# Where a small side job is woven into a large kernel: the sampled tokens' heads move from the first MLP to the second, and the first blocks' head outputs are transposed one stage earlier

## The chip, the core and the metric

The kernel runs on one core of one Trainium2 chip. The metric is device microseconds of one execution, lower being better; the kernel before took 2691.82 us, the median of three runs (2685.82 to 2694.05).

Engines by short names: PE is TensorE, which multiplies matrices; PEld its weight loads; DVE is VectorE, ACT is ScalarE, POOL is GpSimd, SP is the sync engine. SP, ACT and POOL can issue DMA transfers, and an engine's instructions run in the order of its own queue.

## What is computed

One step of a one-layer decoder with two kinds of heads side by side, over a prompt of 2048 tokens and, separately, over 8 × 4 sampled tokens that carry a state. Cut to what matters:

```python
def decoder_layer(x, p, lp, state):
    xn = rms_norm(x, lp['norm_mix_pre'])
    qk_raw, v_m, o_m, gates, q_a, k_a, v_a = split_projection(xn @ lp['w_in'])
    qk, conv_new = short_conv(qk_raw, conv_buf, lp['conv_w'])
    q, k, v, ig, lf = mlstm_heads(qk, v_m, gates, lp['b_gates'])
    if state is None:      # prompt: 16 chunks of 128 tokens
        (c_new, n_new, m_new), h = mlstm_prompt(q, k, v, ig, lf)
        att = swa_prompt(q_a, k_a, v_a, lp['attn_sinks'])
    else:                  # sampled tokens: one chunk of 4, from the state
        (c_new, n_new, m_new), h = mlstm_chunk(init, (q, k, v, ig, lf))
        att, k_new, v_new = swa_sample(q_a, k_a, v_a, k_buf, v_buf, lp['attn_sinks'])
    mix = concatenate([mlstm_output(h, o_m), rms_norm(att)]) @ lp['w_out']
    x = x + rms_norm(mix, lp['norm_mix_post'])
    u = rms_norm(x, lp['norm_ffn_pre'])
    f = square(relu(u @ lp['w_up'])) @ lp['w_down']
    x = x + rms_norm(f, lp['norm_ffn_post'])
    return x + sigmoid(x @ lp['w_pgate']) * (p @ lp['w_pproj'])
```

The mLSTM heads ("memory heads") carry a matrix c (64 × 128 for each of 4 heads), a vector n of 64 and a number m; the attention heads look back 128 tokens, with a key and value cache for the sampled tokens.

## The kernel before

**Stages.** The 16 blocks of 128 prompt tokens are first projected in six chunks (`project`, L615, called at the loop ahead of L1350): gates, keys and values, then queries, the q/k path, and at the end the `v` and the `o` columns, each as eight products per block (one for each 128 rows of the model width). The sampled tokens ride along with the last chunk; their rows go to a DRAM buffer `zsd`. The last blocks then go on in three groups of two chunks each (`GROUPS`): the output projection (`mix_load`, `mix_mm`, `mix_post`), the MLP (`mlp`, 16 steps of 256 hidden columns), and the gated embedding. The head outputs of each block are two DRAM tiles `yd[b]`, written by the heads (`mlstm_chunk` L893, `swa_chunk` L980) and read again by `mix_load`.

Every f32 operand is held as a high and a low part, and one product is three matmuls (`mm3`). Weights go through a ring (`Ring`): the first time a tile is loaded raw, cast on ACT (L248), its low part taken on POOL or DVE (L249), and, if it is used again, kept in DRAM (`keep`, a POOL store `wk<-w`, L268); later uses reload it (`w<-wk`, SP, L274). Which tile is loaded when is written down in `plan` (L383).

**FAST.** MLP step s of group gi is "slow" for s < `FAST[gi]` (L56: 4, 2, 2): 48 matmuls for each of the two chunks, 96 in all. From `FAST[gi]` on it is "fast": `up_both` (L1632) makes both chunks together from seven products of half the size and sums of them, 84 matmuls. The sums of the activations (`sums`, L1585, `last_sum`, L1618, on DVE and ACT) are made once in a group, in step `FAST[gi] − 1`, in memory (`tp`, `wide`) that is taken over there from the load buffers and from decode. The combined weights are made once (`product`, L284 and L413) and kept; a slow step's own weights have keys of their own.

**The side jobs.** `Flow` (L127 on) fixes PE's order while the program is written. It counts a clock of its own in planned microseconds: each matmul adds its columns (times its passes) divided by 2400. Side jobs are generators that issue some work and yield the planned time until they are due again; between products, `tick` (L164) lets those go on that are due, and `drain` (L180) issues all that is left. `swa` and `mls` are the prompt's heads, `tsp` the loads and transposes, `dec` the sampled tokens' heads: `decode` (L1341) waits `DECW` = 20 and then runs `decode_mlstm` (L1070) and `decode_swa` (L1256), whose tiles share memory. Only PE's order (and that of the cache copies, L1089) is kept as written; instructions of other engines may be put ahead in their queues when what they need is there. `reuse_waits="tile"` means that a tile waits for those that held its memory before.

**Around the change.** After the last `project` comes `pe.drain(swa)` (L1350), then the first group's loads are added and drained at once (L1516 and 1517: six y loads on SP, `MIXW` = 6 planned microseconds, then for each of three blocks four transposes and the splits), and only then `mix_mm(0, 0)` begins. `decode` is added at L1543, ahead of the loop over the groups, so it starts in group 0's second output projection (`mix_mm(0, 1)`) and is drained in step `FAST[0] − 1` = 3 (L1724 and 1725). Its loads are issued by ACT (`fetch_small`, L201), among them for each half e and head h

```python
fetch_small(cs[er, :, h, 0:128], c_in[e, h])
fetch_small(cs[er, :, h, 128], n_in[e, h])
```

(L1211 and 1212), where the second writes the 64 elements of n to 64 partitions for four samples; its stores (`put`) go through POOL, and the two copies of the caches (L1089) through SP.

## Time and profile before

| | |
|---|---|
| median of three runs | 2691.82 us |
| profiled execution, its span | 2687.73 us, 2685.6 us |
| last `o` products of the last projection end | 675 us |
| first output projection (`mo`) starts | 693.2 us |
| MLP of group 0: first `up`, first fast step (4) | 797.5 us, 986.1 us |
| second output projection, MLP of group 1 | 1478.7 us, 1549.3 us |
| fast steps of group 1 | 1620.8 us on |

Times are from the start of the span of one profiled execution. A row of a group or of the timeline has the engine, the line of the code, what is written and read (`dn<-w,hh` is a tile `dn` made from `w` and `hh`, buffer numbers left out) and behind "x" a count. In brackets stands how long the engine was idle before, and what ended the wait. A row that ends in "q", such as SPq or ACTq, is an engine's queue at work on issuing DMAs. Names of tiles: `mo` output projection, `up` and `dn` the MLP's two products, `y` loaded head outputs, `yt` and `ut` their transposed forms, `re`, `hh`, `hl` the hidden values, `f` the sums over the MLP, `ts`, `tl` the sums for the fast steps; decode's tiles begin with `dp` and `da` on PE (`dpk`, `daS` and so on), or with `s` (`scs` is c and n, `skc`, `svc` the caches, `szqa` the queries), and `cb` is its constants.

### The profile page before, as it was taken

Reading aid. Unit: us, or ns where it says so; the run is one execution under the profiler, and the core shown is the slowest. Engines: PE = TensorE matmul, PEld = TensorE weight load, DVE = VectorE, ACT = ScalarE, POOL = GpSimd, SP = SyncE. Lnnn points to the kernel's source line nnn. Section 1 sums busy time; section 2 is a strip of 40 time slices with the busy share of each in tenths; the row PEclk is TensorE's granted clock in tenths of the full one; section 3 lists DMA queues with packets and bytes.
Section 4 is the critical chain, followed back from the end, with each engine's and each line's share of the span. In section 5 each row is a group of like instructions: output and inputs, shape, how many; then the busy total and the mean of one; then the engine's idle time right before and its main releaser. Section 6 shows DMA issues by size and latency. Waiting matters only on the chain.

```text
span 2685.6 us, 39181 instructions
## 1 busy us (share of the span) xinstructions
PE 2546.3 (95%) x14282; PEld 2216.1 (83%) x14282; DVE 1473.3 (55%) x3109; ACT 981.4 (37%) x2163; POOL 613.3 (23%) x894
## 2 busy tenths in 40 slices
PE   6899999999878999999989999999999998999997
PEld 6788878887657788888878888899988878999986
DVE  5675756755554486566663474444446345444453
ACT  4555444544433443334452352222223133222241
POOL 5311111112323156566651113000001010000010
PEclk9899999999889999999989999999999999999999
DMA  8756656667977366666589865555556886777786
GB/s 284 275 200 197 208 175 220 210 212 250 287 247 156 133 218 244 235 235 235 227 301 323 322 213 182 187 190 189 188 189 224 293 327 215 255 259 256 258 293 227
DMA packets 225336, 626.97 MB, mean 233 GB/s; under 512 B 35233, under 2 KB 71445, under 8 KB 225128
## 3 DMA queue, kind: packets, MB, share of 16 engines
q1 hardware_dynamic: 173424, 466.78, 52.2%
q0 software_dynamic: 44176, 154.25, 14.8%
q10 hardware_dynamic: 7544, 3.44, 0.6%
q8 instruction: 113, 1.85, 0.3%
q14 instruction: 79, 0.65, 0.1%
HBM read 470.22 MB, written 155.25 MB: 233 GB/s over the span
## 4 chain that ended last, share of the span: by engine, by line
PE 72%; DMA 9%; DVE 8%; issue 4%; POOL 3%; ACT 3%; ACTq 0%; SPq 0%; POOLq 0%; DVEq 0%
PE up L145 19%; PE dn L145 19%; PE pg L145 6%; PE mo L145 4%; PE v L145 3%; PE o L145 2%; PE qk L145 2%; DMA wk<-w 2%; PE gv L145 2%; POOL w L249 2%; PE pv L145 1%; PE aT L149 1%; PE aO L145 1%; DMA w<-wk 1%; PE qa L145 1%
## 5 line engine op out<-in xcount | busy, mean ns | idle before, releaser
L145 PE MATMUL dn<-w,hh 128*128 128x512 f32 x1792 | 567.7, 398 | 14.1 <-DVE f L1683 8.9
L145 PEld LDWEIGHTS dn<-w,hh 128*128 128x128 f32 x1792 | 332.7, 189 | 96.7 <-DVE f L1683 15.4
L1683 DVE TENSOR_TENSOR f<-f,dn 128x512 f32<-128x512 f32 x420 | 285.7, 686 | 218.0 <-PE dn L145 217.7
L145 PE MATMUL dn<-w,hl 128*128 128x512 f32 x896 | 354.3, 395 | 0.1
L1647 DVE TENSOR_TENSOR re<-up,re 128x384 f32<-128x384 f32 (+1 forms) x280 | 144.1, 515 | 297.6 <-PE up L145 297.6
L145 PEld LDWEIGHTS dn<-w,hl 128*128 128x128 f32 x896 | 168.9, 189 | 39.9 <-DVE hl L228 0.6
L268 POOL DMA_DIRECT2D wk<-w x242 | 134.1, 555 | 145.6 <-DVE w L249 109.6
L1648 ACT COPY re<-up 128x384 f32<-128x384 f32 (+1 forms) x40 | 17.9, 448 | 383.1 <-PE up L145 383.1
L228 DVE TENSOR_TENSOR hl<-re,hh 128x384 fp32r<-128x384 f32 (+1 forms) x192 | 117.5, 612 | 65.6 <-ACT hh L227 62.0
L1573 ACT ACTIVATE re<-re 128x384 f32<-128x384 f32 (+1 forms) x160 | 78.8, 493 | 179.3 <-DVE re L1647 177.2
L248 ACT CAST w<-wb 128x512 fp32r<-128x512 f32 x98 | 60.8, 621 | 199.2 <-PE dn L145 124.9
L248 ACT CAST w<-wr 128x512 fp32r<-128x512 f32 (+1 forms) x152 | 93.4, 619 | 104.9 <-issue 30.8
L249 POOL TENSOR_TENSOR w<-wr,w 128x512 fp32r<-128x512 f32 (+1 forms) x76 | 102.0, 1342 | 81.8 <-ACT w L248 62.8
L1394 POOL TENSOR_TENSOR f<-f,gffn 128x512 f32<-128x512 f32 x16 | 21.0, 1319 | 415.4 <-ACT j L1392 415.2
L249 POOL TENSOR_TENSOR w<-wb,w 128x512 fp32r<-128x512 f32 x70 | 89.9, 1295 | 100.8 <-ACT w L248 100.3
L249 DVE TENSOR_TENSOR w<-wr,w 128x512 fp32r<-128x512 f32 (+1 forms) x76 | 80.5, 1061 | 44.4 <-ACT w L248 42.4
L1574 ACT ACTIVATE re<-re 128x384 f32<-128x384 f32 (+1 forms) x192 | 94.8, 494 | 5.9
L1002 DVE CUSTOM_DVE_ANT_0 s<-aS,cst,sink 128x256 f32<-128x256 f32 (+1 forms) x128 | 57.1, 472 | 72.4 <-PE aS L145 72.2
L145 PE MATMUL up<-ut00h,w 128*128 128x384 f32 x320 | 88.6, 348 | 8.4 <-ACT f L1681 5.0
L227 ACT CAST hh<-re 128x384 fp32r<-128x384 f32 (+1 forms) x192 | 92.4, 482 | 6.8
L145 PE MATMUL up<-ut01h,w 128*128 128x384 f32 x320 | 89.8, 343 | 4.8 <-ACT re L1573 4.8
L1008 ACT ACTIVATE s<-s,swt 128x257 f32<-128x257 f32 (+1 forms) x128 | 63.3, 496 | 71.6 <-DVE swt L1005 70.4
(1501 smaller groups left out, 6436.3 us busy)
## 6 DMA issues: line engine op xcount, KB each, us to landing
w<-wk SPq DMA_DIRECT2D x678, 512.0 KB, 4.6
wk<-w POOLq DMA_DIRECT2D x238, 512.0 KB, 5.7
wr<-in_w_down_dram SPq DMA_DIRECT2D x64, 256.0 KB, 5.9
wb<-in_w_up_dram SPq DMA_DIRECT2D x28, 512.0 KB, 3.9
w<-wk SPq DMA_DIRECT2D x20, 528.0 KB, 4.2
x<-in_x_prompt_dram SPq DMA_DIRECT2D x16, 512.0 KB, 4.1
xr<-in_x_prompt_dram SPq DMA_DIRECT2D x16, 512.0 KB, 12.7
y<-yd SPq DMA_DIRECT2D x32, 256.0 KB, 6.2
```

Source lines behind the costliest of these rows:

```text
L145: ins = self.pe.matmul(out, lhsT, rhs, start=start, stop=stop)
L227: act.copy(hi, src)
L228: dve.tensor_tensor(lo, src, hi.bitcast(F32), ALU.subtract)
L248: act.copy(hi, src)
L249: (eng or weng()).tensor_tensor(lo, src, hi.bitcast(F32), ALU.subtract)
L268: put(self.kept[key], t.bitcast(U32))
L1002: dve.tensor_tensor_reduce(s_[:, s, lo : 2 * P], pS[:, s, lo:], bias[:, j, lo:], 1.0 if s == 0 else 0.0625, sink[:, h : h + 1], ALU.add, A ...
L1008: act.activation(e_, e_, AF.Exp, bias=nm[:, s : s + 1], accum_out=sm[:, s : s + 1])
L1573: act.activation(t, src, AF.Relu)
L1574: act.square(t, t)
L1647: add = lambda out, a, b: dve.tensor_tensor(out, a, b, ALU.add)
L1683: dve.tensor_tensor(out(i), out(i), ps[i], ALU.add)
```

## The change

1. `FAST` becomes 2, 4, 2: group 0's steps 2 and 3 are fast, group 1's are slow.
2. `decode` is added at the start of group 1's MLP and drained in that group's step 3.
3. The loads of `decode` go through POOL instead of ACT, and the two cache copies through POOL instead of SP. n is loaded in rows of 64 elements, 16 rows for each half, and transposed on PE into its column; on the way out it is transposed back and stored in rows. Two yields of 1.5 are added for these.
4. In the last projection the y loads of blocks 0, 1 and 2 are issued ahead of the `o` columns into the buffers of x, and their memory halves are transposed between the `o` products, where the other chunks transpose the next x; the window halves, which need no transpose, are split behind the projection. The load and drain at L1516 and 1517 go.

```diff
-FAST = 4, 2, 2
+FAST = 2, 4, 2
...
-    dma, put, fetch_small = nc.sync.dma_start, nc.gpsimd.dma_start, nc.scalar.dma_start
+    dma, put = nc.sync.dma_start, nc.gpsimd.dma_start
...
+        last = ci + 1 == len(CHUNKS)
+        nxt = GROUPS[0][0] if last else CHUNKS[ci + 1]
         for nm, zoff in (("v", Z_V), ("o", Z_O)):
-            if nm == "o" and ci + 1 < len(CHUNKS):
-                fetch(ci + 1)
+            if nm == "o":
+                if last:
+                    ys = [load_y(xpool, "x", b) for b in nxt]
+                else:
+                    fetch(ci + 1)
...
-                if nm == "o" and ci + 1 < len(CHUNKS):
-
-                    nxt = CHUNKS[ci + 1]
+                if nm == "o":
+
                     if k == 3:
                         chunk = Chunk(tpA, f"x{ci + 1}")
                     if k > 3 and k - 4 < len(nxt):
-                        transpose_x(chunk, nxt, k - 4, 0, ps_m)
+                        if last:
+                            mix_heads(chunk, k - 4, nxt[k - 4], ys[k - 4])
+                        else:
+                            transpose_x(chunk, nxt, k - 4, 0, ps_m)
...
+        if last:
+            for i, t in enumerate(ys):
+                mix_windows(chunk, i, t)
         return r
+
+    def load_y(pool_, tag, b):
+
+        src = yds if b == "s" else yd[b]
+        t = pool_.tile([P, D], F32, tag=tag, name=f"y_{b}")
+        for e in range(2):
+            dma(t[: src[e].shape[0], e * 512 : e * 512 + 512], src[e])
+        return t
+
+    def mix_heads(x, i, b, t):
+        transpose_split(t[:, 0:512], *x.part(0, slice(i * P, (i + 1) * P)), ps_m, f"yt{b}", g_mix[0])
+
+    def mix_windows(x, i, t):
+        split_gain(*x.part(1, slice(i * P, (i + 1) * P)), t[:, 512:].rearrange("p (j q) -> p j q", j=4), g_mix[1])
...
-        fetch_small(cb, A["const_b"][:, 0:NCB])
+        put(cb, A["const_b"][:, 0:NCB])
...
-            tc.keep_in_program_order(dma(oc[:, 0 : WIN - DT, :], cc[:, DT:WIN, :]))
+            put(oc[:, 0 : WIN - DT, :], cc[:, DT:WIN, :])
...
-        n_in = A["state_mlstm_n"].rearrange("l (k e) h d -> e h d (l k)", e=2)
+        n_in = A["state_mlstm_n"].rearrange("l (k e) h d -> e (l k) h d", e=2)
...
+        nrow = sp.tile([DB // 2 * MH, 2, MK], F32, name="snr")
         for e in range(2):
             er = slice(e * MK, (e + 1) * MK)
             for h in range(MH):
-                fetch_small(cs[er, :, h, 0:128], c_in[e, h])
-                fetch_small(cs[er, :, h, 128], n_in[e, h])
+                put(cs[er, :, h, 0:128], c_in[e, h])
+            for k in range(DB // 2):
+                put(nrow[k * MH : (k + 1) * MH, e], n_in[e, k])
+        yield 1.5
+        pn = psum(ps_s, "dpn")
+        pe.transpose(pn[:, 0:16], nrow.rearrange("p e d -> p (e d)"), ident[:16, :16])
+        dve.tensor_copy(cs[:, :, :, 128], pn[:, 0:16].rearrange("p (k h) -> p k h", k=4))
         yield 1.5
...
                 put(c_out[e, h], cs[er, :, h, 0:128])
-                put(n_out[e, h], cs[er, :, h, 128])
+        ncol = sp.tile([P, 16], F32, name="snc")
+        dve.tensor_copy(ncol.rearrange("p (k h) -> p k h", k=4), cs[:, :, :, 128])
+        yield 1.5
+        pn = psum(ps_s, "dpno")
+        pe.transpose(pn[:16, 0:P], ncol, ident)
+        dve.tensor_copy(nrow.rearrange("p e d -> p (e d)"), pn[:16, 0:P])
+        for e in range(2):
+            for k in range(DB // 2):
+                put(n_out[e, k], nrow[k * MH : (k + 1) * MH, e])
...
-        fetch_small(kc, A["cache_swa_k"].rearrange("l b s k d -> s (l b) (k d)"))
-        fetch_small(vc, A["cache_swa_v"].rearrange("l b s k d -> s (l b) (k d)"))
+        put(kc, A["cache_swa_k"].rearrange("l b s k d -> s (l b) (k d)"))
+        put(vc, A["cache_swa_v"].rearrange("l b s k d -> s (l b) (k d)"))
...
-    tsp.add(mix_load(0, 0, GROUPS[0][0], False))
-    pe.drain(tsp)
+    yt[0] = chunk
     tsp.add(mix_load(0, 1, GROUPS[0][1], False))
     mix_mm(0, 0, GROUPS[0][0], False)
...
-    dec.add(decode())
...
         G = f"{gi}"
+        if gi == 1:
+            dec.add(decode())
```

The other loads in `decode_mlstm` and `decode_swa` change from `fetch_small` to `put` in the same way, and `mix_load` calls the three new functions.

More of the change, by code (lines that the diff above doesn't have):

```diff
@@ L1078, in decode_mlstm @@
         zqk = sp.tile([NS, 512], F32, name="zqk")
-        fetch_small(zqk, zsd[:, Z_QK : Z_QK + 512])
+        put(zqk, zsd[:, Z_QK : Z_QK + 512])
         zg = sp.tile([NS, 2 * MH], F32, name="zg")
-        fetch_small(zg, zsd[:, Z_G : Z_G + 2 * MH])
+        put(zg, zsd[:, Z_G : Z_G + 2 * MH])
         for b in range(DB):
@@ L1177, in decode_mlstm @@
         pool.memset(va[:, :, 129:130], 0.0)
-        fetch_small(va[:, :, 0:128], zsd[:, Z_V : Z_V + 512].rearrange("p (h v) -> p h v", h=MH))
+        put(va[:, :, 0:128], zsd[:, Z_V : Z_V + 512].rearrange("p (h v) -> p h v", h=MH))
         num = sp.tile([NS, MH, 130], F32, name="snum")
@@ L1224, in decode_mlstm @@
         so = sp.tile([NS, 512], F32, name="sso")
-        fetch_small(so, zsd[:, Z_O : Z_O + 512])
+        put(so, zsd[:, Z_O : Z_O + 512])
         act.activation(so, so, AF.Tanh, scale=0.5)
@@ L1258, in decode_swa @@
         bias_s = sp.tile([P, nk], F32, name="bias_s")
-        fetch_small(bias_s, A["const_b"][:, NCB : NCB + nk])
+        put(bias_s, A["const_b"][:, NCB : NCB + nk])
         zqa = sp.tile([NS, 512], F32, name="zqa")
-        fetch_small(zqa, zsd[:, Z_QA : Z_QA + 512])
+        put(zqa, zsd[:, Z_QA : Z_QA + 512])
         zkv = sp.tile([NS, 256], F32, name="zkv")
-        fetch_small(zkv, zsd[:, Z_KA : Z_KA + 256])
+        put(zkv, zsd[:, Z_KA : Z_KA + 256])
         y = sp.tile([NS, 512], F32, name="sya")
@@ L1442, in mix_load @@
             yt["s"] = sp2.tile([P, KT, 2 * NS], F32R, tag="s", name="sy2")
-        todo = [(i, b, lp.tile([P, D], F32, tag="ld", name=f"y_{b}"), yd[b]) for i, b in enumerate(c)]
+        todo = [(i, b, load_y(lp, "ld", b)) for i, b in enumerate(c)]
         if sample:
-            todo.append((None, "s", lp.tile([P, D], F32, tag="ld", name="y_s"), yds))
-        for i, b, t, src in todo:
-            for e in range(2):
-                dma(t[: src[e].shape[0], e * 512 : e * 512 + 512], src[e])
+            todo.append((None, "s", load_y(lp, "ld", "s")))
         yield MIXW
-        for i, b, t, _ in todo:
+        for i, b, t in todo:
             if i is None:
```

12 lines of the change are left out of this document (6 added, 6 removed).

## The prediction

> **What bounds the kernel now.** I read the page first, then PE's waits around the seam between projection and MLP, then a table of stretches, and last the chain of waits and single rows.
>
> ```profile
> span 2685.6 us, 39181 instructions
> PE 2546.3 (95%) x14282; PEld 2216.1 (83%) x14282; DVE 1473.3 (55%) x3109; ACT 981.4 (37%) x2163; POOL 613.3 (23%) x894
> ```
>
> TensorE (PE) is busy for 95% of the span, so the kernel is bound by PE, and only time in which PE stands still or runs at a low clock can be won. The question is where the missing 139 us (2685.6 − 2546.3) lie. PE's waits between 676 and 955 us, the seam and the first MLP steps of group 0 (line, what it waited for: total, times, longest):
>
> ```profile
> PE mo L145 <- DMA w<-wk: 13.4, 1, 13.4
> PE mo L145 <- ACT f L1486: 6.6, 1, 6.6
> PE up L145 <- ACT f L1681: 5.0, 1, 5.0
> PE up L145 <- ACT re L1573: 4.8, 1, 4.8
> PE up L145 <- POOL w L249: 3.4, 1, 3.4
> ```
>
> The same stretch as a table: after the length come the busy times of PE, PE's weight loads, VectorE (DVE), ScalarE (ACT) and GpSimd (POOL), then the granted clock, the DMA share and GB/s. (From 742 to 756 nothing is lost.) The last three rows are ten fast steps of group 0 (4 to 13), and of group 1 step 0 and the thirteen fast steps 2 to 14.
>
> ```profile
> 675.00:693.00 18.00, 11.27 (x78) 8.59 (x77) 10.03 (x31) 7.86 (x23) 8.09 (x12) 0.68 0.97 363
> 693.00:742.00 49.00, 44.95 (x188) 34.33 (x187) 29.41 (x51) 19.84 (x39) 18.62 (x24) 0.94 0.90 263
> 756.00:770.00 14.00, 0.60 (x4) 0.16 (x2) 3.70 (x3) 2.12 (x6) 3.66 (x3) 0.65 0.52 125
> 770.00:797.00 27.00, 20.40 (x78) 15.68 (x79) 9.29 (x40) 9.45 (x19) 7.21 (x9) 0.80 0.74 261
> 797.00:855.00 58.00, 52.51 (x305) 42.99 (x303) 35.35 (x89) 27.91 (x62) 18.93 (x30) 0.98 0.73 184
> 855.00:952.00 97.00, 87.86 (x426) 73.77 (x427) 40.53 (x69) 34.26 (x74) 21.70 (x26) 0.94 0.46 125
> 986.00:1310.00 324.00, 316.03 (x1561) 280.96 (x1560) 200.65 (x270) 131.41 (x241) 202.16 (x221) 1.00 0.64 243
> 1549.00:1587.00 38.00, 36.91 (x193) 32.55 (x193) 34.49 (x58) 23.83 (x44) 3.37 (x6) 1.00 0.67 223
> 1621.00:2029.00 408.00, 408.00 (x2028) 366.31 (x2027) 184.87 (x301) 92.33 (x177) 18.64 (x21) 1.00 0.56 187
> ```
>
> For each row I count as lost the length minus the busy time, plus the busy time times (1 − clock). The first two rows lose 6.7 + 3.6 and 4.1 + 2.7, together 17.1 us: the **seam**. The next four lose 13.6, 10.7, 6.5 and 14.4, together 45.2 us: **decode** (the sampled tokens' heads) beside group 0. Group 1's MLP, which runs without decode, loses 1.1 us in step 0 and nothing in its fast steps. What makes decode so dear shows in what the SP queue waited for, and then in the chain of waits (start, length, what):
>
> ```profile
> SPq L274 <- DMA scs<-in_state_mlstm_n_dram: 26.9, 3, 23.3
> ```
>
> ```profile
> 742.07 10.81 DMA cb<-in_const_b_dram
> ...
> 765.45 4.77 DMA scs<-in_state_mlstm_n_dram
> 770.28 7.53 DMA w<-wk
> ```
>
> The n state is fetched with the head's 64 elements across partitions, 4 bytes apiece. SP's reload of a weight tile (L274) stood 23.3 us behind one such fetch, and PE stood 13.4 us for that tile. The loads of decode are issued by ACT, which meanwhile evacuated nothing: the 6.6 us behind ACT L1486.
>
> **The change, part by part.**
>
> *Seam.* These rows carry it (SP, then PE):
>
> ```profile
> 679.88 4.91 SPq L1448 DMA_DIRECT2D y<-yd  x6
> ...
> 689.75 1.09 PE L149 MATMUL yt0t<-ident,y 128*128 128x128 f32 x4 [2.52 <-DMA y<-yd]
> ...
> 693.19 1.20 PE L145 MATMUL mo<-w,yt00h 128*128 128x512 f32 x2
> ```
>
> Now the first y loads go out only at 679.88, after the projections, and the first landed for 689.75. After the change these six loads stand in the last o projection, before 660, on SP ahead of w_out's loads; the three groups of transposes are only moved (same count), and their splits go onto DVE and ACT, which have room there. The window splits read chunk part 1 and come behind the last o product, but part 1 is first read in the second half of the first output block, 36 products later. So `mo` follows the window attention's last product, about when SP issues its next loads, and starts near 681 instead of 693.2; the last products of the memory heads, ahead of it now, fall among its own. Late next: blocks 3 to 5. Their loads take the very place on SP that y0 to y2 had (679.88), so the first can land near 689.75, while PE, 6 planned us (MIXW) into `mo`, asks for it near 687. I leave 2.5 us for that and 1.5 for the rest: 17.1 − 4 = **13 won**; bounds 8 (block 3 waits as long as block 0 did and the clock falls again) and 17 (all).
>
> *Decode leaves group 0.* The 45.2 us go. Left are group 1's 1.1 us and about as much for the first making of the weights: **43 won**, bounds 35 and 45. Decode's own PE work leaves group 0 and comes back in group 1, where PE is as full, so it cancels; the two short transposes of n that are new are below 1 us.
>
> *FAST.* Steps 2 and 3 become fast in group 0 and slow in group 1. Step parts, from the chain (`up` x96 is a slow step's, x84 a fast one's; `dn` is the same for both):
>
> ```profile
> 1587.42 16.84 PE up L145 x96
> 1604.27 16.70 PE dn L145 x72
> ```
>
> A slow step is 33.5 us; group 1's fast one 408/13 = 31.4; group 0's, which also makes the products, 324/10 = 32.4. Group 0 wins 2 × 1.1, group 1 loses 2 × 2.1: **2 lost**, with as many products in all. The cover in group 0 is POOL, 202 of 324 us busy in the fast steps; if it were gone, the weights would end last, as they do there already for 0.8 us a step.
>
> *Decode's loads change queues.* Thirty-two loads from ACT and two cache copies from SP go to POOL, and n is fetched in rows of 256 bytes and transposed. What would be late is a PE transpose that waits for a landing, with `up` and `dn` queued behind it in PE's fixed order. Rows that bear on it (POOL's idle time in brackets):
>
> ```profile
> 639.73 3.09 POOL L1085 DMA_DIRECT2D out_dram<-zsd  x6
> ...
> 875.34 2.53 ACTq L1272
> ...
> 1597.37 1.28 POOL L298 TENSOR_TENSOR wb<-wb,wb 128x512 f32<-128x512 f32 x1 [39.23 <-DMA wb<-in_w_up_dram]
> ```
>
> The decode puts of line 1085 ran at 639.73, some 100 us ahead of decode's first load at 742.07: what isn't PE's is put forward where its queue is free. POOL stood idle for 39.23 us just where decode now begins, and is busy 3.4 of 38 us in group 1's step 0. At 0.52 (the six puts in 3.09) to 2.53 us each, the 34 cost POOL 18 to 86 us of the 139 that these four steps last. So the first loads are hidden. The attention half's loads can't be put forward, as they reuse the memory half's tiles and stand behind its 16 stores: (16 + 5) × 0.52 is 11 us, and a landing like the 4.77 of scs makes 16, against 16.5 planned us until its first transposes. I take 3 us (0 to 8). In the Trainium skill, the page "DMA: Bandwidth & Descriptors", section "Latency and other measured facts", gives a first byte after about 0.6 us for loads from SP or ACT and about 1 us for POOL's, which speaks against the move. Thirty-two loads by that would be an estimated 13 us if each were exposed; no row here shows the two side by side.
>
> *Decode's end against step 3.* Adding up the planner's own clock: at group 1's step 3, whose start drains decode, 116 planned us have passed since the MLP's start, and decode, which now starts with the MLP (before, in the second half of the output projection, some 45 us earlier), needs 125. What is issued bare is its last tail, with this chain in the trace of before:
>
> ```profile
> 914.20 1.18 ACT L1312 ACTIVATE sss<-sss,sst 128x1056 f32<-128x1056 f32 x1
> ...
> 923.18 2.09 PE daO L145 x18
> ...
> 929.57 0.94 DVE L1596 TENSOR_TENSOR ts<-ut01h,ut00h 128x768 f32<-128x768 f32 x1
> 969.76 1.82 DVE L1630 TENSOR_TENSOR ut01l<-tl,ut01h 128x768 fp32r<-128x768 f32 x2
> ```
>
> PE stands through max, exponential (1.18) and the copies between the last transposes and that product: **4 us** (3 to 8). The sums for the fast steps begin 4 us after decode's last product (929.57 after 923.18 + 2.09) and took until 971.6, 42 us; before, step 4 came 57 us after them, now 33.5 + 2. Of the 42, 26 are the sums' own DVE time (28 operations of 0.94), and product 7, the first to need the last of them, is the fourth of the step, 6 us in. I take 2 us (0 to 8), and 2 (0 to 15) for what I don't see, such as ACT and DVE crowded by decode beside a full PE. Together 3 + 4 + 2 + 2 = **11 lost** in group 1; all lower ends give 3, all upper ends 39.
>
> The sum: −13 − 43 + 2 + 11 = **−43 us**. The profiled execution took 2687.73 us around its span of 2685.6; the median of the three runs, 2691.82, lies 4.1 above it. So 2644.7 for an execution like the profiled one, and **2649 us** as the median.
>
> The clock is half of the seam's story: behind the gap of 13.4 us the clock reads 0.65, then 0.80. By the Trainium skill's page "TensorE: Matmul & The Clock Gate", Part 1, an idle window of about 3.4 us halves the clock until about as long of work, and these rows agree; by it the bare tail, if it is over 3.4 us in one piece, costs an estimated 1.7 us more than I take.
>
> **The rivals.** *(a) Part of the stalls travels.* ACT and DVE do decode's small steps beside a PE that has no slack, and POOL's queue holds the weight splits of steps 2 and 3 behind stores that wait. Half of 45.2, 23 us, in place of the 11, and the seam's lower bound: −8 − 43 + 2 + 23 = −26, so 2666; with 29 of stall, 2672. For it: PE's waits on ACT L1573 and POOL L249 stand in the rows from 797 on, when the n fetches of 765 were past. Against it: POOL's stores of n, single elements too, ran then, and are rows now.
>
> *(b) Slower.* If the loads on POOL aren't put forward but issued where they are used, PE stands for each of six landings (hrow, v, n with c, zqa, kc, vc) at the 10.81 us that cb took: 65 us. −13 − 43 + 2 + 65 = +11, 2703. It decides from 54 us of new stalls on. Against it stands the row at 639.73; for it, that POOL's queue is one line, and one store that waits holds all loads behind it. The Trainium skill's figures above point the same way, but by far less.
>
> *(c) Everything is won.* Seam 17, decode 45, the 2 of FAST, and only the 3 in group 1: −57, 2635. For it: group 1's steps have no lost time.
>
> *(d) The early y loads bring nothing*, because blocks 3 to 5 take over the whole wait: −8 − 43 + 2 + 11 = −38; inside the forecast's range.
>
> **How the numbers follow.** Forecast with (d) 0.65, (a) 0.17, (b) 0.07, (c) 0.11. The forecast's own cases reach from 2635 to 2668 (the upper end with 30 of the 39 us in group 1); to hold 8 in 10, I go from 2632 to 2676, which takes in (c) and (a) and leaves out (b) and the tails. A difference of 0.3%, 8 us, is about what a measurement of this kernel can tell from no change. Faster by more than that: (a), (c) and the forecast without their worst tails, 0.89; within it 0.05, from the tail of (a) and a mild (b); slower 0.06, from (b).
>
> **What would show it.** Right: `mo` starts near 681 with no cold rows behind it; the stretch from `mo`'s start to group 0's step 4 loses under 10 us; no SP wait over 5 us on scs; group 0 has fourteen steps of about 32.4; in group 1, steps 0 to 2 grow by decode's PE work and a gap of 3 to 5 us stands just ahead of step 3's first `up`. Wrong: a PE wait of over 5 us on skc, szqa, snr or scs; group 1's step 4 starting with a gap behind DVE ts; PE waiting on POOL w L249 in group 1.

## The result and the profile after

The changed kernel takes 2694.48 us against 2686.42 for the kernel before (medians of 20 runs each, taken in turn on the same chips): ratio 1.0025, interval 1.0017 to 1.0033. It is 8 us slower where 43 us less were forecast, within the 0.3% that the prediction set as the least that can be told from no change, though the interval itself leaves out 1. The profiled execution took 2696.58 us, its span 2694.8. The page of the kernel after, whole span:

```profile
span 2694.8 us, 39194 instructions
PE 2550.8 (95%) x14284; PEld 2221.0 (82%) x14284; DVE 1475.1 (55%) x3112; ACT 982.1 (36%) x2163; POOL 635.4 (24%) x928
```

PE is busy as before, and 144 us are missing in place of 139. That hides two large movements, which a table of stretches shows. Of the kernel before, group 0's first MLP steps and its output projection, then the same two in group 1:

```profile
693.20:797.50 104.30, 80.25 (x341) 62.11 (x340) 53.94 (x116) 39.02 (x78) 30.95 (x41) 0.88 0.79 245
797.50:986.10 188.60, 173.96 (x898) 147.14 (x897) 104.52 (x195) 77.24 (x160) 55.81 (x70) 0.96 0.57 158
1478.70:1549.30 70.60, 70.60 (x326) 57.76 (x325) 33.56 (x61) 25.17 (x52) 12.62 (x15) 1.00 0.88 316
1549.30:1683.60 134.30, 133.21 (x674) 119.13 (x673) 85.68 (x131) 54.56 (x100) 33.90 (x38) 1.00 0.57 196
```

The same work in the kernel after (seam, output projection, step 0, steps 1 to 3; then group 1's output projection, step 0, steps 1 to 3):

```profile
694.20:710.70 16.50, 9.93 (x68) 7.39 (x66) 12.83 (x33) 7.27 (x18) 6.44 (x8) 0.65 0.98 369
710.70:784.50 73.80, 72.68 (x331) 58.92 (x330) 41.61 (x76) 34.88 (x74) 32.91 (x40) 0.99 0.85 299
784.50:832.20 47.70, 41.80 (x193) 35.38 (x192) 40.19 (x62) 28.15 (x52) 13.32 (x18) 0.89 0.67 234
832.20:930.90 98.70, 97.05 (x481) 86.63 (x480) 63.21 (x82) 39.57 (x73) 55.78 (x60) 1.00 0.62 228
1421.70:1504.70 83.00, 74.38 (x325) 60.02 (x324) 33.93 (x62) 25.53 (x53) 25.54 (x41) 0.94 0.85 290
1504.70:1543.20 38.50, 38.09 (x203) 33.05 (x202) 23.19 (x72) 22.82 (x46) 4.03 (x7) 1.00 0.71 207
1543.20:1693.60 150.40, 139.46 (x708) 116.12 (x707) 75.76 (x148) 45.28 (x98) 22.62 (x33) 0.93 0.27 84
```

Group 0, from the first `mo` to step 4, took 292.9 us (104.3 + 188.6) and takes 220.2: 72.7 won, decode's own PE work among it. Group 1, over the same steps, took 204.9 and takes 271.9: 67.0 lost. The span grew by 9.2. It comes together from the start, +17.6 (the last chunk's first `o` product at 670.38 in place of 652.76); the last `o` part and the seam, −0.1; group 0, −72.7; group 1, +67.0; and −2.6 for the rest.

**Where the 17.6 us at the start come from.** POOL's timeline of the kernel after, and PE's first transposes in it:

```profile
5.82 0.53 POOL L1113 DMA_DIRECT2D out_dram<-in_cache_swa_k_dram  x1
27.36 0.56 POOL L1113 DMA_DIRECT2D out_dram<-in_cache_swa_v_dram  x1
```

```profile
25.57 1.12 PE L149 MATMUL x00t<-ident,x 128*128 128x128 f32 x4 [25.57 <-DVE x L584]
```

The same row of the kernel before:

```profile
14.36 1.11 PE L149 MATMUL x00t<-ident,x 128*128 128x128 f32 x4 [14.36 <-DVE x1t L498]
```

In the kernel before the two cache copies (496 KB each) stood on SP at 741 and 766, held there by `keep_in_program_order`. The change moved them to POOL and dropped that hold. They need nothing that the kernel makes, so they went to the very front, among the first loads of x and w_in.

**Group 1.** PE's waits of the kernel after from 1421 to 1700 (line, what it waited for: total, times, longest):

```profile
PE dn L145 <- DVE f L1718: 8.1, 1, 8.1
PE mo L145 <- ACT f L1521: 6.8, 1, 6.8
PE daT L149 <- ACT sss L1350: 2.7, 1, 2.7
```

The second is explained by two rows, of ACT's timeline and of POOL's:

```profile
1458.88 0.63 ACT L1256 ACTIVATE sso<-sso 32x512 f32<-32x512 f32 x1 [10.20 <-DMA sso<-zsd]
```

```profile
1453.38 0.54 POOL L1255 DMA_DIRECT2D sso<-zsd  x1
```

This is decode's gate tanh. It was put forward in ACT's queue, ahead of the evacuations of `mo`, and stood there 10.20 us for a load that POOL had issued at 1453.38, behind decode's other loads. The first wait is in step 3. DVE's timeline there, from the first of an unbroken run of sums to the accumulation behind it:

```profile
1668.55 0.95 DVE L1637 TENSOR_TENSOR ts<-ut11h,ts 128x768 f32<-128x768 f32 x1
...
1678.10 0.95 DVE L1662 TENSOR_TENSOR tl<-ut11l,ut11l 128x768 f32<-128x768 f32 x1
1678.97 0.68 DVE L1718 TENSOR_TENSOR f<-f,dn 128x512 f32<-128x512 f32 x1
```

The accumulation into `f` frees the PSUM tile (where products are summed) for the next `dn`, and it stood behind ten microseconds of sums for the fast steps.

**The seam.** PE's waits of the kernel after from 676 to 712:

```profile
PE mS L145 <- DVE m14f L906: 3.9, 1, 3.9
PE aR L145 <- DVE num L973: 2.3, 1, 2.3
```

The y loads no longer hold PE there, but these two waits of the memory heads do, with the clock at 0.65 in the stretch that begins at 694.20.

### The profile page after: what moved, and what is told of

It is laid out like the page before. It is cut to its first block, busy times and chain, and to the rows that moved or that the text cites. A ratio compares the mean times of both kernels' runs of the same rounds, so it can differ in the third digit from the quotient of the medians.

```text
span 2694.8 us, 39194 instructions
## 1 busy us (share of the span) xinstructions
PE 2550.8 (95%) x14284; PEld 2221.0 (82%) x14284; DVE 1475.1 (55%) x3112; ACT 982.1 (36%) x2163; POOL 635.4 (24%) x928
## 4 chain that ended last, share of the span: by engine, by line
PE 68%; DVE 9%; DMA 7%; issue 7%; POOL 5%; ACT 3%; SPq 0%; POOLq 0%; DVEq 0%; ACTq 0%
PE dn L145 18%; PE up L145 18%; PE mo L145 5%; PE pg L145 4%; PE v L145 3%; PE o L145 2%; POOL w L249 2%; PE qk L145 2%; PE gv L145 2%; PE qa L145 1%; PE aT L149 1%; PE aO L145 1%; DMA wk<-w 1%; DVE hl L228 1%; PE aS L145 1%
## 5 line engine op out<-in xcount | busy, mean ns | idle before, releaser
L145 PE MATMUL dn<-w,hh 128*128 128x512 f32 x1792 | 572.3, 401 | 22.6 <-DVE f L1718 16.9
L1608 ACT ACTIVATE re<-re 128x384 f32<-128x384 f32 (+1 forms) x160 | 78.8, 493 | 170.6 <-DVE re L1682 168.3
L145 PE MATMUL up<-ut11h,w 128*128 128x384 f32 x320 | 88.8, 340 | 0.0
L1615 POOL CAST hh<-hh 128x16 fp32r<-128x16 f32 x32 | 7.1, 222 | 338.2 <-ACT hh L227 338.1
```

The lines of the kernel that those rows point to most:

```text
L145: ins = self.pe.matmul(out, lhsT, rhs, start=start, stop=stop)
L1608: act.activation(t, src, AF.Relu)
```

## The experiments

All ran the whole computation. The ratio is to the kernel before on the same chip. Two places are read in each profile: when the last chunk's first `o` product starts, and the stretch from group 0's first `mo` to group 2's, which holds everything of decode and nothing of the start. The e kernels ran on one chip, the b, c and g kernels on a second, the d and f kernels on a third; so across letters the stretch is read first, and the ratio for what it says on one chip. Each stretch is that of one execution. The one of the kernel before belongs to an execution of 2687.73 us, while this kernel's medians on the three chips went from 2677.4 to 2685.5; a stretch set against that row can so be out by several microseconds, and where the medians of one chip say less, both are given.

| kernel | ratio, interval | last `o` | stretch |
|---|---|---|---|
| before | 1 | 652.8 | 1465.0 |
| after | 1.0025, 1.0017 to 1.0033 | 670.4 | 1455.5 |
| e1_copies | 1.0002, 0.9988 to 1.0016 | 652.8 | 1448.8 |
| e2_tanh | 1.0011, 1.0000 to 1.0022 | 670.1 | 1445.2 |
| e3_early | 0.9977, 0.9966 to 0.9989 | 668.3 | 1434.4 |
| e4_noy | 1.0071, 1.0049 to 1.0092 | 669.2 | 1456.5 |
| b_copies | 1.0046, 1.0032 to 1.0060 | 667.6 | 1455.9 |
| b_nrows | 0.9981, 0.9968 to 0.9994 | 647.0 | 1464.6 |
| c1_all | 0.9905, 0.9888 to 0.9923 | 659.5 | 1430.1 |
| c2_late | 0.9838, 0.9820 to 0.9855 | 647.6 | 1421.2 |
| d_noy | 0.9888, 0.9865 to 0.9912 | 649.8 | 1428.4 |
| d_actq | 0.9871, 0.9848 to 0.9893 | 648.9 | 1427.0 |
| d_group0 | 0.9882, 0.9860 to 0.9905 | 652.1 | 1426.5 |
| d_winlate | 0.9872, 0.9847 to 0.9897 | 654.4 | 1422.2 |
| d_notanh | 0.9910, 0.9889 to 0.9930 | 653.7 | 1432.9 |
| f_late | 0.9967, 0.9953 to 0.9980 | 644.4 | 1448.1 |
| f_rows | 0.9945, 0.9925 to 0.9966 | 651.3 | 1448.6 |
| f_pool | 0.9917, 0.9898 to 0.9936 | 654.7 | 1432.8 |
| g_place | 0.9999, 0.9987 to 1.0012 | 652.7 | 1466.5 |
| g_early | 0.9987, 0.9978 to 0.9997 | 649.0 | 1465.1 |

### Undoing one suspect at a time in the changed kernel

**e1_copies**

```diff
-            put(oc[:, 0 : WIN - DT, :], cc[:, DT:WIN, :])
+            tc.keep_in_program_order(put(oc[:, 0 : WIN - DT, :], cc[:, DT:WIN, :]))
```

> The changed kernel, with the two cache copies (still on POOL) held behind the POOL instruction traced ahead of them, as they were on SP before; nothing else is edited. With the copies gone from the start, SP's order of loads there is that of the kernel before again. Theory (the start is slow because the copies, put forward to 5.8 and 27.4 us, share the DMA engines with the first x and w_in loads, and with them SP's order changed): first transposes back from 25.6 to about 14.4 us, the first o product of chunk 0 from 130.3 back to about 113, the time about 17 us below the changed kernel's, so about 9 below the kernel before (ratio 0.997). Rival (the start's loss comes from other parts of the change, as the loads of the decode or the y tiles in the schedule): the first transposes stay above 20 us and the time stays within 4 us of the changed kernel's.

The last chunk's row, PE's timeline:

```profile
652.80 0.63 PE L145 MATMUL o<-w,x5h 128*128 128x512 f32 x2
```

The start is back where it was before (652.76), and the first transposes are at 14.09 for the 14.36 of the kernel before, so the theory holds there; that the `o` row agrees to a tenth is chance, as what follows shows. The medians moved by less: 1.0002 against 1.0025, 6 us with intervals of 2 to 4 on each side. The profiled execution (2672.97) was the fastest of this kernel's twelve, so its span overstates the gain. The hold put the copies only behind a store that itself was put forward, so they now ran at 591 and 643, in the projection, whose last chunk took 106.5 us from `o` to `o` (546.3 to 652.8) in place of 99.2, which took back what the chunks ahead of it had won.

**e2_tanh**

```diff
-        act.activation(so, so, AF.Tanh, scale=0.5)
+        tc.keep_in_program_order(act.activation(so, so, AF.Tanh, scale=0.5))
```

> The changed kernel, with the decode's gate tanh (the ACTIVATE on sso) held behind the ACT instruction traced ahead of it, so that it can't be put forward between the evacuations of group 1's output projection. The loads stay where they were put forward to: POOL's and SP's orders are unchanged. Theory (ACT's queue was blocked by that instruction's wait for its load): PE's wait of 6.8 us on ACT's evacuation f of mo goes, with the cold products behind it; group 1's output projection takes 73 us in place of 83, and the time falls by 8 to 12 us, to about 2684. Rival (the decode loads themselves crowd the DMA engines there, DMA share 0.95): PE waits as long on another load or evacuation, and the time falls by less than 3.

Group 1's output projection of that kernel:

```profile
1421.10:1497.50 76.40, 73.26 (x326) 59.59 (x325) 33.51 (x61) 25.17 (x52) 25.40 (x41) 0.96 0.93 315
```

6.6 us shorter, and PE's wait on ACT is gone. A wait of 3.1 us for a weight tile is left, at a DMA share of 0.93, so the rival may have the remainder. The medians give 4 us (1.0011 against 1.0025), with intervals about as wide.

**e3_early**

```diff
-        if gi == 1:
-            dec.add(decode())
...
         tsp.add(mix_post(*part[0]))
+        if gi == 1:
+            dec.add(decode())
         mix_mm(*part[1])
```

> The changed kernel, with decode added ahead of group 1's second output projection block (some 45 us earlier, where group 0 had it before) in place of the MLP's start; FAST and the queues as changed. Theory (decode ends too late: its last part is drained bare and DVE makes the sums among step 3's accumulations): no gap ahead of step 3's first up and none of 8.1 us on DVE f in step 3, which takes 33 to 35 us in place of 46.8; some of it is paid in the mix, 0 to 6 us. In all 6 to 13 below the changed kernel, about 2684. Rival (what decode costs beside a full PE is the same wherever it stands): steps 1 to 3 get shorter and the mix and step 0 longer by the same, time within 3 us of the changed kernel's.

Its output projection of group 1, and its steps 0 to 3:

```profile
1417.00:1500.70 83.70, 74.15 (x336) 59.26 (x335) 39.83 (x96) 29.19 (x60) 26.10 (x42) 0.94 0.86 287
1500.70:1669.00 168.30, 168.30 (x901) 142.75 (x900) 93.00 (x186) 64.64 (x136) 26.83 (x39) 1.00 0.39 122
```

Steps 0 to 3 took 188.9 us (38.5 + 150.4) and take 168.3, with no idle time at all and the full clock; the output projection pays 0.7. In the medians 13 us (0.9977). Of the 20.6 us, what stood idle was 11 (2.66, 8.10 and less); the rest was the clock, 0.93 in those steps before.

**e4_noy**

The changed kernel with the y loads and transposes behind the projection again:

```diff
+    tsp.add(mix_load(0, 0, GROUPS[0][0], False))
+    pe.drain(tsp)
-    yt[0] = chunk
```

> The changed kernel without the early y loads: the first blocks' head outputs are loaded and transposed behind the projections, as before; everything else as changed. Theory (the seam's gain was eaten: y's splits stand on DVE ahead of the memory heads' operations, and PE waits for those): from the last o product to the first mo about 18 us in place of 16.5, the o phase 22 in place of 24, so the time within 3 us of the changed kernel's. Rival (the seam was won as predicted, and what it won is lost later on): 10 to 13 us above the changed kernel's, about 2706.

From the first `o` of the last chunk, then group 0's output projection:

```profile
669.20:709.90 40.70, 33.75 (x218) 25.96 (x216) 22.68 (x72) 18.97 (x50) 17.00 (x24) 0.87 0.83 289
709.90:789.60 79.70, 75.77 (x331) 59.48 (x330) 46.49 (x81) 35.18 (x70) 30.07 (x37) 0.96 0.92 292
```

The changed kernel takes 40.3 for the first and 73.8 for the second. By these rows neither theory is right: the seam proper wins 0.4, but the output block behind it, in which only blocks 3 to 5 are then left to load and split, 5.9. Together 6 us of the 13 forecast. The medians gave 12, in the rival's range of 10 to 13, but with an interval of some 6 us on each side; a second run of the same pair, below, gives 5.9 in these two parts again.

### One part alone on the kernel before, and the edits together

**b_copies** changes L1089 of the kernel before as the change does (`put`, no hold) and nothing else.

> The kernel before, with one part of the change alone: the two cache copies are issued by POOL and are no longer held behind what is ahead of them. Theory (the copies are what slows the start): they run in the first 40 us, and the first o product of the last chunk comes about 17 us later than 652.8; group 0's first output block, from which they are gone, gets 0 to 10 us shorter (104.3 before). Net 7 to 17 us slower than the kernel before. Rival (the changed kernel's start is slow for another reason): the last chunk's o starts within 5 us of 652.8.

PE's first transposes, and group 0's output block (the two views of this kernel):

```profile
25.55 1.11 PE L149 MATMUL x00t<-ident,x 128*128 128x128 f32 x4 [25.55 <-DVE x L584]
```

```profile
707.80:796.20 88.40, 80.00 (x341) 61.75 (x340) 53.45 (x113) 37.55 (x75) 30.45 (x41) 0.92 0.94 277
```

The loss of the start comes with this one line: 14.8 of the 17.6 us (last `o` at 667.6). Not expected was the size of the other half: with the copies off SP's queue, group 0's output block is 15.9 us shorter though decode is still in it (by the ratio the time grew by 12 us where the start alone lost 15, so the medians put that gain lower). SP's first loads are also in another order than in the kernel before; whether their order or the copies' traffic costs the 15 us wasn't separated.

**b_nrows** fetches n in rows on the kernel before (loads still on ACT), as the change does, and stores it as before.

> The kernel before, with one part of the change alone: the state n is fetched in rows of 256 bytes and transposed (still on ACT's queue, and stored as before); decode stays beside group 0. Theory (the element-wise fetches of n are what held SP's weight reload for 23.3 us and PE for 13.4): SP's wait on scs goes, the output projection of group 0 takes 85 to 92 us in place of 104.3, and the time falls by 12 to 20 us. Rival (the other loads of decode and the copies, all in the same stretch, hold SP as long): the wait moves to another load, and the time falls by less than 5.

What SP's queue waited for from 676 to 955:

```profile
SPq L274 <- DMA scs<-in_state_mlstm_c_dram: 21.3, 1, 21.3
```

The rival is right: the wait of 23.3 us behind n is now one of 21.3 behind c, which is loaded in long rows. The output block took 99.8 in place of 104.3, and later steps gave it back (step 1 63.1 for 59.3, step 4 39.6 for 32.2). So it isn't the shape of the fetch that holds SP. What does stands in the program's own list of waits, here SP's of the kernel before around the first copy:

```
L274 DMA w_8351<-wk_7965 128x1024 [waits DMAHW4_49,PE_49]
L1089 DMA out_dram<-in_cache_swa_k_dram 8x15872 [waits DMAHW6_49]
L274 DMA w_8353<-wk_7972 128x1024 [waits DMAHW5_49,DMAHW4_49,PE_49]
L1089 DMA out_dram<-in_cache_swa_v_dram 8x15872 [waits DMAHW5_49]
L274 DMA w_8432<-wk_7997 128x1024 [waits DMAHW6_49,PE_49]
```

and ACT's loads of the same time:

```
L1211 DMA scs<-in_state_mlstm_c_dram 64x4x128 [waits DMAHW5_49]
L1212 DMA scs<-in_state_mlstm_n_dram 64x4x1 [waits DMAHW6_49]
L1211 DMA scs<-in_state_mlstm_c_dram 64x4x128 [waits DMAHW7_49]
L1212 DMA scs<-in_state_mlstm_n_dram 64x4x1 [waits DMAHW0_49]
```

Eight completion counters, DMAHW0 to 7, go round over all transfers that SP and ACT issue, and, as the list reads, a transfer is issued only when the last user of its counter has landed. A weight reload on SP thus waits for whichever decode load on ACT had its counter last. POOL's transfers have eight of their own (DMASW0 to 7). How the copies come into it isn't shown: SP's issue of the two took 0.79 and 0.68 us.

**c1_all** holds the copies, holds the tanh and adds decode early; **c2_late** differs from it in that the copies are written behind decode's last stores:

```diff
                 put(n_out[e, k], nrow[k * MH : (k + 1) * MH, e])
+        for out, cache in ((12, "cache_swa_k"), (13, "cache_swa_v")):
...
+            tc.keep_in_program_order(put(oc[:, 0 : WIN - DT, :], cc[:, DT:WIN, :]))
```

> The changed kernel with three edits together: the copies held behind the POOL instruction ahead of them, the gate tanh held behind the ACT instruction ahead of it, and decode added ahead of group 1's second output projection block. Theory (three separate losses that pay back group 0's gain): they add up, 6 to 17 + 4 + 13, so 23 to 34 us below the changed kernel, about 2663 (ratio to the kernel before 0.988 to 0.993). Rival (one place of congestion, met in turn): no more than the best single edit brings, about 2676 (0.997).

> As the kernel with the three edits, but the copies are issued behind decode's last store of n, which waits for decode's results, so that they run in group 1's MLP; in the other they were put forward to the fifth and sixth chunk of the projection, where that chunk took 106.5 us in place of 100. Theory: the last chunk is back at 99 to 101 us, 4 to 7 us below the other; group 1's steps, at a DMA share of 0.3, lose nothing to the copies, and the attention half's loads behind them come 1 us later. Rival (the copies cost PE as much wherever they run): same time as the other within 3 us.

c1_all took 2658.86 and c2_late 2639.80 against 2682.00 for the kernel before: the losses do add up, and c2_late, 42 us below, is faster than both kernels by far. (Its near twin d_winlate, on another chip, is 34 below.) The step between the two, 19 us, is more than the 4 to 7 expected. The projection gives 11.9 (last `o` at 647.6, 659.5 in c1_all), and 6.3 come from group 0's step 0, a place where the two do the same work. c1_all's step:

```profile
774.00:821.70 47.70, 41.80 (x192) 35.37 (x192) 40.18 (x61) 28.09 (x52) 13.33 (x18) 0.89 0.67 234
```

and c2_late's:

```profile
761.40:802.80 41.40, 37.46 (x193) 32.36 (x191) 39.04 (x61) 28.02 (x52) 14.29 (x17) 1.00 0.72 259
```

The one has idle gaps of 2.25 and 0.83 us at its head and reads a clock of 0.89, the other one gap of 1.00 there and keeps the clock. The 2.25 has a chain behind it. Of c1_all, POOL's, DVE's and PE's rows:

```profile
781.57 0.54 POOL L1467 DMA_DIRECT2D x1d<-f  x1 [4.16 <-issue]
```

```profile
782.74 2.74 DVE L1438 SCALAR_TENSOR_TENSOR f<-f,ms,xr 128x512 f32<-128x512 f32 x4 [2.58 <-POOL ms L1444]
```

```profile
786.06 0.50 PE L145 MATMUL dn<-w,hl 128*128 128x512 f32 x1 [2.25 <-DVE hl L228]
```

and POOL's of c2_late:

```profile
766.03 0.54 POOL L1470 DMA_DIRECT2D x1d<-f  x1 [1.22 <-DVE ms L1446]
```

POOL stands 4.16 us ahead of a store, for nothing that the profile shows; DVE waits for POOL's `ms` behind it, and PE for DVE. This isn't chance. All six kernels with decode beside group 1 whose copies run ahead of group 0 (the changed kernel, the four e kernels and c1_all) have these three waits (4.16 or 4.17, 2.57 to 2.59, 2.25 or 2.26) in this step, which takes 44.2 to 47.9 us; none of the seven whose copies run later (c2_late, the d kernels but d_group0, the g kernels) has them, and their step takes 41.5 to 43.1. So the early copies cost here once more; what POOL waits for stays open.

### Parts of the best kernel undone

**d_noy**, **d_actq**, **d_group0** and **d_winlate** are c2_late without the early y loads; with decode's loads issued by ACT; with decode beside group 0 and `FAST = 4, 2, 2`; and with the window splits of y behind `pe.drain(swa)`. **d_notanh** is c2_late without the hold on the tanh.

> The kernel with the three edits and the late copies (2639.8 us, 0.984 of the kernel before), without the early y loads: the first blocks' head outputs are loaded and transposed behind the projections, as before. It measures that part alone, where the earlier run without it (on the changed kernel) gave 6 us in the profiled stretch and 12 in the medians. Theory (half of what was forecast for the seam is won, the rest is eaten by the splits of y that stand on DVE ahead of the memory heads' operations): 5 to 9 us slower than with it. Rival 1 (all 13 us are won): 11 to 15 slower. Rival 2 (nothing is won): within 3.

> The kernel with the three edits and the late copies, with decode's loads issued by ACT again, as before; the order of PE's work is the same. Theory (in group 1 the loads are put forward on either queue and nobody waits for them; the queue is worth only the ACT time of 32 issues of about 0.6 us): 0 to 5 us slower, most of it in group 1's output projection. Rival (POOL's queue is what made decode cheap): ACT's queue holds the evacuations behind loads that wait for their tiles, PE waits on ACT f and hh, and the time rises by 10 to 25.

> The kernel with the three edits and the late copies, with decode beside group 0 again (added ahead of its second output projection block) and FAST 4, 2, 2 as before; queues, rows of n, copies and the early y loads as in that kernel. Theory (decode is dear in group 0 because PE there waits for freshly made weights, with ACT, DVE and POOL making them; leaving it is worth most of the 43 us): 20 to 35 us slower. Rival (it was dear because of its copies, its n fetches and the queue that they held, so it is as cheap there once these are gone): within 8 us.

> The kernel with the three edits and the late copies, with the splits of y's window half written behind the last window attention in place of ahead of it, so that on DVE the memory heads' operations (reciprocal, kw, the masked products) come ahead of most of them. Theory (those splits are what PE waits for at the seam, 3.9 us ahead of mS and 2.4 ahead of aR): from the last o product to the first mo 11 to 14 us in place of 16.5, the time 2 to 5 us lower. Rival (the memory heads' own chain of dependent operations is as long): the seam stays over 15.5 and the time within 2 us.

> The kernel with the early decode and the late copies, but with the gate tanh free to be put forward in ACT's queue again; only 12 rows of ACT's and 20 of DVE's order differ. Theory (ACT's queue stands behind that instruction's load): group 1's output block 82 to 84 us in place of 76.7, 4 to 8 us slower than with the hold (0.984 of the kernel before). Rival (the wait is for DMA share, and the hold only moves it): within 3 us.

d_noy: from the last chunk's first `o` to the end of group 0's output block 119.7 us, 113.8 with the early loads: 5.9, the theory's range; by the ratios 13, but d_winlate, which has the early loads and ran on the same chip, is only 4 us below d_noy. d_winlate: PE's wait moved from `mS` to `mX`, 4.0 us, and the seam is 15.4 in place of 16.5, just under the rival's 15.5 and far from the theory's 11 to 14: the memory heads' own chain is about as long. (Its time wasn't measured beside c2_late's on one chip.) d_notanh: group 1's output block 86.7 in place of 76.7, somewhat more than the theory said (by the ratios 19 us, of which the start of the profiled execution has 6):

```profile
1399.30:1486.00 86.70, 76.48 (x336) 61.33 (x335) 39.95 (x97) 29.19 (x61) 26.14 (x42) 0.92 0.84 277
```

d_actq: 5.8 more in the stretch, just over the theory's 5, though SP waits 31 us in sum behind c and the bias from 1385 to 1640: PE has no wait for a weight tile in that time, only 3.5 on DVE and 3.0 on ACT. d_group0 is the surprise. The theory wanted 20 to 35 us; the stretch is 5.3 longer, and the time 3 us above d_winlate's on the same chip (12 by the ratio to c2_late's): the rival. With its queues mended, decode is almost as cheap beside group 0.

### Which part took decode's cost beside group 0

**f_late**, **f_rows** and **f_pool** go from the kernel before towards d_group0 step by step: the copies behind decode's stores on POOL; n in rows as well; the loads on POOL as well.

> The kernel before, with one edit: the two cache copies leave SP's queue and are issued by POOL behind decode's stores of n, which wait for decode's results. Decode stays beside group 0, its loads on ACT, n element by element. Theory (the copies on SP's queue, between the weight reloads, are the dearest part of decode): group 0's output block 85 to 92 us in place of 104.3, the start as before, the time 12 to 20 us below the kernel before (0.9925 to 0.9955). Rival (the element-wise fetches of n hold SP, as the prediction read it): SP's wait on scs stays, the block stays over 98 us and the time falls by less than 6.

> The kernel before with the copies late and n fetched and stored in rows of 256 bytes, loads still on ACT, decode beside group 0, no early y loads. Theory (copies and n are met one after the other, and each hides the other's worth): another 6 to 12 us below the kernel with the copies late alone. Rival (the rows bring nothing, as alone): within 4 us of it.

> As that one, with decode's loads on POOL; PE's order is the same. Theory (the queue matters little, as in the run with ACT's queue in group 1, 8 us by the ratios): 0 to 8 us below the one on ACT. Rival (in group 0, where ACT makes the weights and evacuates, a load that waits at the head of ACT's queue costs PE its evacuations): 10 to 20 us below.

The stretch as one row of each kernel, before, f_late, f_rows, f_pool, d_group0 and c2_late:

```profile
693.20:2158.20 1465.00, 1406.37 (x6845) 1216.88 (x6844) 783.28 (x1271) 498.65 (x964) 423.81 (x489) 0.98 0.66 227
```

```profile
684.50:2132.60 1448.10, 1401.41 (x6845) 1213.50 (x6844) 784.30 (x1271) 498.92 (x964) 426.20 (x491) 0.99 0.66 229
```

```profile
691.30:2139.90 1448.60, 1404.00 (x6848) 1213.11 (x6847) 787.11 (x1274) 497.49 (x964) 425.10 (x491) 0.99 0.65 229
```

```profile
694.40:2127.20 1432.80, 1400.23 (x6847) 1210.89 (x6846) 796.25 (x1274) 498.90 (x964) 443.50 (x523) 0.99 0.65 232
```

```profile
692.40:2118.90 1426.50, 1395.03 (x6848) 1207.98 (x6847) 788.99 (x1269) 498.27 (x968) 446.42 (x526) 0.99 0.65 232
```

```profile
687.90:2109.10 1421.20, 1392.13 (x6848) 1207.53 (x6847) 785.85 (x1269) 499.24 (x968) 451.22 (x526) 1.00 0.66 233
```

The copies off SP: 16.9, where the medians of one chip say 9 (5 to 13). Rows of n: nothing here (−0.5), 6 us in the medians within intervals as wide, so theory and rival stay undecided. The loads off ACT: 15.8, the rival's 10 to 20, where the medians say 7.5, the theory's 0 to 8. The three together are 32 in the stretch and 22 in the medians. The early y loads and the tanh's hold: 6.3. The place: 5.3 here, 4.3 against d_winlate, 3 by the medians of one chip, which isn't clear of the noise. One view shows what the queue does to SP: its longest wait behind a decode load was 23.3 us before; in f_late it is

```profile
SPq L359 <- DMA zqa<-zsd: 18.1, 1, 18.1
```

and with the loads on POOL SP waits for none. PE is another matter. In f_late and f_rows it has no wait for a reloaded weight tile from its first `mo` on for 300 us. In f_rows its longest waits there are on DVE (4.8 and 3.6), and it stands idle for 24 us, in f_pool for 13. So SP's waits behind the counters are shown, and so is the gain, but not that the one makes the other: ACT's own queue, where the loads stood among the evacuations, is as open. By the Trainium skill's page "DMA: Bandwidth & Descriptors", section "Issuing engines are not separate DMA queues", issuing from several engines saves only the issuing time. Here moving 32 loads from one issuer to another is worth 15.8 us of the stretch (7.5 by the medians) with PE's order the same. ACT's rows of issuing them add up to 26 us of its queue in f_rows, so the issuing time alone could cover the gain; how much of it the counters have isn't shown.

**g_place** and **g_early** move decode in the kernel before, with `FAST = 2, 4, 2`, and leave all else: at the MLP's start, and ahead of the second output block.

> The kernel before with the move alone: decode is added at the start of group 1's MLP and FAST is 2, 4, 2; the loads stay on ACT, the copies on SP and held, n element by element, no early y loads. The stretch from group 0's first output product to group 2's is 1465.0 in the kernel before. Theory 1 (the move and the queues are two ways to the same gain: in group 1 SP's reloads are few and DMA share low, so SP and ACT lose little by what is queued there): group 0 wins its 70 us, group 1 pays some 60 of them, as in the changed kernel with its late decode, 1450 to 1458, time 0.994 to 0.998. Theory 2 (what is in the queues costs as much beside group 1): 1464 to 1480, time 1.000 to 1.006.

> As that one, with decode added ahead of group 1's second output projection block, so that it ends ahead of step 3. Theory 1: 15 to 21 us below it, stretch 1430 to 1440, time 0.985 to 0.991: the move alone would then be worth 25 to 35, provided that decode starts early enough. Theory 2: the copies and the fetches of n meet the weight reloads of group 1's output block as they met those of group 0's, PE waits for w again, and it is over 1450, 0.994 or more.

PE's waits of g_place from 1385 on:

```profile
PE mo L145 <- DMA w<-wk: 9.8, 1, 9.8
PE dn L145 <- DVE f L1684: 8.1, 1, 8.1
PE up L145 <- DMA w<-wk: 6.3, 1, 6.3
PE dpk L149 <- DMA skc<-in_cache_swa_k_dram: 4.8, 1, 4.8
```

Theory 2 holds: 0.9999 and 0.9987, stretches of 1466.5 and 1465.1 against 1465.0. The waits of group 0 turn up beside group 1, the one on `w<-wk` among them. The move alone is worth nothing, or at most the 3.5 us of g_early's ratio.

## Why the prediction was wrong

**"Decode leaves group 0: 43 won, 11 lost in group 1" is the step that failed.** It took the idle time in which decode stood as decode's cost, and held that it would go with decode. Group 0 did get 72.7 shorter, but group 1 got 67.0 longer, and the move alone (g_place, g_early) brings 0 to 3.5 us. What decode cost beside group 0 goes without moving it: taking the copies off SP's queue and the loads off ACT's, and n in rows, is worth 22 us in the medians (32 in the stretch); the place itself is then worth 3 to 5. Beside group 1 the loads' queue still counts, with 5.8. Rival (a), that the stalls travel, was right in kind and too small in price. In sum: between the −43 of the forecast and the +9.2 of the span lie 52.2, of which seam and both groups, −43 in the forecast and −5.8 measured, are 37.2, the start 17.6 and the rest −2.6.

**The reading of the n fetch failed with it.** The row of 23.3 us behind n was read as the fetch's shape; with rows, c had the wait (21.3).

**The queues.** That what isn't PE's is put forward where its queue is free was read off a row and used only to the change's credit. That did bring the first loads early, as forecast: PE waited on none of skc, szqa, snr or scs. But it also put forward what the change had let loose: the copies to the start (+17.6, a term that the sum didn't have, and up to 6.3 more in group 0's step 0), and the tanh into group 1's output block (6.6 undone in e2_tanh and 10.0 in d_notanh, of the 12.4 by which it grew). Rival (b) priced loads that are issued too late; these two losses came from work that is issued too early.

**Decode's end against step 3** was seen, with nearly the right gap (2.7 for 3 to 5) and the right rows, but 8 us were taken for what cost up to 20.6 in steps 0 to 3 (13 in the medians of e3_early): the sums didn't come late to the products, they stood ahead of the accumulations in DVE's queue, and the clock fell behind each gap.

**The seam:** 13 forecast, 6 measured in two pairs of profiles, below the lower bound of 8 (4 to 13 by the medians), and in another place: `mo` still starts 16.5 us after the last `o`, as the memory heads' own chain is about as long as the y loads were, and what is won is won in the output block.

**FAST** as forecast: group 0's steps 2 and 3 went to 32.3 us each. **The sum:** with the three losses mended, c2_late stands at 0.9838 (0.9820 to 0.9855), 42 us below the kernel before, where 43 were forecast. That is luck, an agreement by size only: the parts are others.

## What to carry to other kernels

An idle stretch beside a side job tells where the cost falls, not what causes it: before pricing a move, look at which queue the waiting engine stands behind and what is in that queue, since that moves along. When an instruction loses its fixed place, ask where it can go at the earliest, and who waits there; a transfer that needs nothing goes to the start, and a cheap operation whose input comes late blocks everything behind it. Undo the parts one by one and also make the main part alone: here a change that measured as nothing was 42 us faster than the kernel before once three losses were mended.

## What the runs showed of the hardware

Short waits close together can cost more than themselves, but need not. In c1_all's step 0 gaps of 2.25 and 0.83 us, both within 5.3 us, were followed by this row of the table of stretches:

```profile
790.00:794.00 4.00, 4.00 (x15) 3.41 (x15) 1.42 (x3) 1.53 (x3) 0.53 (x1) 0.50 0.55 190
```

In e3_early gaps of 2.25 and 1.03, as close together and at the same products, left the clock at 1.00; its row at the same distance from the step's start:

```profile
798.30:802.30 4.00, 3.87 (x22) 3.27 (x22) 2.78 (x6) 2.62 (x5) 0.53 (x1) 1.00 0.55 188
```

In the same way a later gap of 1.9 in all three was followed by 0.62 in c1_all and by 1.00 in c2_late and e3_early. The step takes 41.6 us without the 2.25, 44.2 with it at the full clock, and 47.9 in c1_all, where the clock falls; what decides between the last two isn't shown. By the Trainium skill's page "TensorE: Matmul & The Clock Gate", Part 1, it takes an idle window of about 3.4 us; here no single gap was that long, yet the clock fell, as it did in the changed kernel behind the gap of 2.66 ahead of step 3 (0.54 and 0.50 in the next two stretches of 4 us).

The start differs from kernel to kernel, though the copies' edits alone change what runs in it: the last chunk's first `o` came between 644.4 and 654.7 us in the 13 kernels whose copies run behind the projection, one execution of each, and between 667.6 and 670.4 in the five that have them at the start.
